# Output projection of the first block: seven block products in the place of eight, with sums of operands

## The chip, the cores and the metric

The kernel runs on one NeuronCore of a Trainium2 chip. The metric is the device time of one execution in microseconds (us), median over runs. Engines are named as in the profile: PE is TensorE (matmuls), DVE VectorE, ACT ScalarE, POOL GpSimd, SP SyncE, which only issues transfers here.

## The reference

Two transformer-like blocks over 512 tokens of width 1024, in float32. What matters here is the end of the first block: the mixed output `y` of its two attention branches is projected by `w_out` (1024 x 1024) and added to the residual `x`, and a normalised copy of the sum feeds a perceptron of hidden width 4096.

```python
y = gates[..., :D_MODEL] * y_a + gates[..., D_MODEL:] * y_b
x = x + y.astype(x.dtype) @ w_out[l]
h2 = rms_norm(x, norm_mlp_g[l])
x = x + jnp.square(jax.nn.relu(h2 @ w_up[l])) @ w_down[l]
```

## The kernel before

Each float32 operand of a matmul is split into a rounded part and its remainder (`hi` by a cast on ACT, `lo` by a subtraction on DVE), and a product is the sum of three matmuls: hi by hi, hi by lo, lo by hi. So a 128-row step of a 128 x 512 output block is three matmuls of 512 columns.

The heads of the second attention branch (`stick(h)`, h = 0 to 7) come one after the other; their work on DVE, ACT and PE is interleaved with matmuls of projections. When a head is done its row block of `y` is split into `T` (tiles `hh`, `hl`). The last head's split is the last thing that the output projection needs: in the trace it is the row L259 at 482.16.

The output projection is `wo(0)` and `wo(1)`: two halves of 512 columns, each over four token blocks (`tb`) of 128 rows and eight steps of 128 along the inner dimension. A half loads four weight tiles `wr` of 512 KB (`load_w`, L133), splits them (L137, L138), and for each token block runs 24 matmuls (L149 to L151) into one of two PSUM banks `mm`. `evac` loads the residual `x` of the token block (L1133) into a tile `qd` of the perceptron's space and adds the product (L1134). After the second half, `do(tb)` of `prep` normalises the finished token block: two squares with a running sum on ACT (L279), two small operations on POOL (L293, L115), two scalings on DVE (L283), then eight transposes of 128 x 128 on PE and their split (L258, L259) into `TM`, which `up(0)` reads. `up(0)` is run in two halves of 256 tokens.

The perceptron's pools (`st`, `b2`) are opened when those of the attention are closed; a tile in them takes space that attention tiles held, and its first write waits for their last readers. The tiles `wx` of this pool hold the first sums of weights of `down2`, which already runs as seven block products: `seven` computes a 2 x 2 block matrix product with seven block products, where some weight operands are sums of blocks. Such a sum is made by transfers: SP loads one block into a tile (`piece`, L181), and POOL issues a transfer that adds the next block to it (`plus`, L185).

A scheduler puts the instructions of each engine into one order ahead of time; an engine works its list strictly in that order. POOL's list holds both the adding transfers and the small operations of `do`.

Of the kernel before, what the change touches and what calls it, by code (L numbers as in the profile page):

```python
# [8 lines left out]
F32 = mybir.dt.float32  # L9
F32R = mybir.dt.float32r  # L10
# [3 lines left out]
ALU = mybir.AluOpType  # L14
# [3 lines left out]
P = 128  # L18
S = 512
D = 1024  # L20
NT = S // P
# [38 lines left out]
class Kern:  # L60
# [132 lines left out]
            nc.vector.tensor_tensor(lo, raw, hi.bitcast(F32), ALU.subtract)  # L193
        return [(hi[:, k, :], lo[:, k, :]) for k in range(2)]

    def seven(self, blk, aop, acc, wx):

        nc = self.nc
        X = []

        def w_of(name):
            out = []
            for q in range(2):
                if name == "X":
                    t = self.piece(blk(0, 0, q), wx())
                    self.plus(t, blk(0, 1, q))
                    X.append(t)
                elif name == "Y":
                    t = X[q]
                    self.plus(t, blk(1, 1, q))  # L210
                elif name == "Z":
                    t = X[q]
                    self.plus(t, blk(1, 0, q))
                elif name == "V":
                    t = self.piece(blk(0, 1, q))
                    self.plus(t, blk(1, 1, q))
                else:
                    t = self.piece(blk(int(name[0]), int(name[1]), q))
                out += self.split_w(t)
            return out  # L220

        def prod(ps, a, w, t, first):
            c = slice(t * P, (t + 1) * P)
            for k in range(4):
                (ah, al), (wh, wl) = (a[0][:, k, c], a[1][:, k, c]), w[k]
                kw = dict(stop=True, skip_group_check=True)
                nc.tensor.matmul(ps, ah, wh, start=(first and k == 0), **kw)  # L227
                nc.tensor.matmul(ps, ah, wl, start=False, **kw)  # L228
                nc.tensor.matmul(ps, al, wh, start=False, **kw)  # L229

        c = [None, None]
        x = [None, None]
        plan = [("X", "5", x, True, (1, 1, ALU.add)), ("11", "3", x, False, (0, 1, ALU.add)),
                ("00", "1", c, True, (0, 0, ALU.add)), ("Y", "6", c, False, (0, 1, ALU.subtract)),
                ("10", "2", x, True, (0, 0, ALU.add)), ("V", "7", c, False, (1, 1, ALU.subtract)),
                ("Z", "4", c, False, (1, 0, ALU.add))]
        for wn, an, bank, first, (i, j, op) in plan:
            w = w_of(wn)
            a = aop(an)
            for t in range(2):  # L240
                if first:
                    bank[t] = self.pmm() if bank is x else self.psum("xa")
                prod(bank[t], a, w, t, first)
                with self.tc.high_priority(EVP):
                    acc(i, t, j, bank[t], op)


    def new_T(self):
# [480 lines left out]
def block1(K, xd, prm, win, wout, wup, wdown, bif, gmix, gmlp, out, gnext):  # L729
# [383 lines left out]
    with ExitStack() as ctx:  # L1113
# [9 lines left out]

        def xt(tb, c):
            return x1[tb // 2][:, tb % 2 * 2 + c, :]
        TM = [[K.quad(F32R) for _ in range(2)] for _ in range(2)]
        do = K.prep(gmlp, wk2, wk2, TM)

        def wo(c):
            def evac(tb, ps):  # L1130
                w = slice(c * S, (c + 1) * S)
                t = xt(tb, c)
                nc.sync.dma_start(out=t, in_=xd[tb * P:(tb + 1) * P, w])  # L1133
                nc.vector.tensor_tensor(t, ps, t, ALU.add)  # L1134
                if c == 1:
                    do(tb, [xt(tb, 0), xt(tb, 1)])
            K.gemm_b(wout[:, c * S:(c + 1) * S], evac, x=K.pairs(T))
        wo(0)
        wo(1)
        K.hT = K.pairs(TM)  # L1140
        hid = {}

# [122 lines left out]
```

## Time and profile before

| | us |
|---|---|
| median of 3 runs (lowest, highest) | 1822.29 (1821.57, 1823.52) |
| the profiled execution's own time | 1821.35 |
| its span, first to last instruction | 1819.6 |
| PE busy in the span | 1781.9 (98%) |
| DVE busy | 1081.0 (59%) |
| ACT busy | 856.0 (47%) |
| POOL busy | 168.7 (9%) |

The profiled execution stands 0.94 us under the median of the runs. "Busy" counts a matmul from start to its modelled end, and matmuls overlap, so a busy PE is read by the distance of the starts of its rows.

### The profile page before, as it was taken

How to read it: one execution, taken by the hardware profiler on the slowest of the kernel's cores; microseconds unless marked ns; L12 is line 12 of the kernel's file. 1: busy time of each engine (PE TensorE's matmuls, PEld its weight loads, DVE VectorE, ACT ScalarE, POOL GpSimd, SP SyncE). 2: the span in 40 equal slices, each digit the busy share in tenths (PEclk: the TensorE clock that was granted, in tenths of full speed). 3: DMA queues.
4: the chain of work that ended last, by engine and by line, in shares of the span. 5: the costliest groups of instructions: out<-in, count | busy, mean ns of one | idle time of the engine just before them, and what ended most of it. 6: DMA issues, size and time to landing. Idle time of an engine off the chain costs nothing.

```text
span 1819.6 us, 29429 instructions
## 1 busy us (share of the span) xinstructions
PE 1781.9 (98%) x11600; PEld 1460.7 (80%) x11600; DVE 1081.0 (59%) x2186; ACT 856.0 (47%) x1701; POOL 168.7 (9%) x223
## 2 busy tenths in 40 slices
PE   7999999999899999999999999999999999999998
PEld 5777788787698888878888888878878888888886
DVE  5375445546555756588475676766364748577744
ACT  4556634343333433355344444766344335376641
POOL 1001111020000101012000001100120000111002
PEclk9999999999999999999999999999999999999999
DMA  7342332221533938378323223232342321332222
GB/s 217 72 105 77 92 93 65 75 93 46 162 117 93 232 106 217 93 185 250 108 82 94 81 85 121 93 116 81 106 147 88 121 76 60 122 128 76 82 70 93
DMA packets 114322, 201.05 MB, mean 110 GB/s; under 512 B 9600, under 2 KB 20224, under 8 KB 114184
## 3 DMA queue, kind: packets, MB, share of 16 engines
q1 hardware_dynamic: 105480, 182.40, 32.0%
q0 software_dynamic: 8704, 16.78, 5.2%
q8 instruction: 91, 1.49, 0.3%
q14 instruction: 47, 0.39, 0.1%
HBM read 184.45 MB, written 14.70 MB: 109 GB/s over the span
## 4 chain that ended last, share of the span: by engine, by line
PE 92%; DMA 3%; ACT 2%; DVE 2%; issue 0%; SPq 0%; POOL 0%; DVEq 0%; POOLq 0%; ACTq 0%
PE mm L151 23%; PE mm L150 23%; PE mm L149 23%; PE xc L638 2%; PE xa L602 2%; PE xa L228 1%; PE xa L227 1%; PE xa L229 1%; PE mm L227 1%; PE mm L228 1%; PE mm L229 1%; PE xc L1066 1%; PE xa L1048 1%; PE xb L624 1%; PE xc L498 1%; PE xa L443 1%
## 5 line engine op out<-in xcount | busy, mean ns | idle before, releaser
L149 PE MATMUL mm<-wh,hh 128*128 128x512 f32 (+1 forms) x896 | 349.6, 391 | 10.0 <-DVE qd L1134 4.8
L138 DVE TENSOR_TENSOR wl<-wr,wh 128x1024 fp32r<-128x1024 f32 (+1 forms) x240 | 288.6, 1211 | 114.8 <-PE mm L150 70.7
L150 PE MATMUL mm<-wl,hh 128*128 128x512 f32 (+1 forms) x896 | 349.4, 390 | 1.2 <-DVE wl L138 1.2
L151 PE MATMUL mm<-wh,hl 128*128 128x512 f32 (+1 forms) x896 | 348.6, 393 | 0.0
L137 ACT CAST wh<-wr 128x1024 fp32r<-128x1024 f32 (+1 forms) x240 | 246.7, 1037 | 120.6 <-PE mm L151 56.4
L149 PE MATMUL mm<-hh,wh 128*128 128x512 f32 x640 | 253.6, 396 | 1.4 <-ACT pg L803 1.4
L151 PE MATMUL mm<-hh,wl 128*128 128x512 f32 x640 | 252.3, 394 | 1.5 <-DVE wl L138 1.4
L150 PE MATMUL mm<-hl,wh 128*128 128x512 f32 x640 | 252.3, 394 | 0.0
L149 PEld LDWEIGHTS mm<-wh,hh 128*128 128x128 f32 x896 | 170.1, 190 | 44.5 <-DVE qd L1134 5.2
L150 PEld LDWEIGHTS mm<-wl,hh 128*128 128x128 f32 x896 | 170.1, 190 | 34.8 <-DVE wl L138 2.5
L151 PEld LDWEIGHTS mm<-wh,hl 128*128 128x128 f32 x896 | 168.8, 190 | 31.9 <-DVE hl L259 0.7
L151 PEld LDWEIGHTS mm<-hh,wl 128*128 128x128 f32 x640 | 120.2, 188 | 28.1 <-DVE wl L138 2.7
L149 PEld LDWEIGHTS mm<-hh,wh 128*128 128x128 f32 x640 | 120.2, 188 | 27.5 <-ACT pg L803 2.7
L150 PEld LDWEIGHTS mm<-hl,wh 128*128 128x128 f32 x640 | 120.4, 188 | 24.6
L115 POOL TENSOR_TENSOR sm<-sm,nhalf 128x4 f32<-128x4 f32 (+1 forms) x64 | 59.0, 922 | 506.6 <-DVE sm L507 329.9
L149 PE MATMUL mm<-qd,wh 128*128 128x512 f32 (+1 forms) x288 | 105.5, 366 | 0.0
L150 PE MATMUL mm<-qd,wh 128*128 128x512 f32 (+1 forms) x288 | 105.4, 366 | 0.0
L151 PE MATMUL mm<-qd,wl 128*128 128x512 f32 (+1 forms) x288 | 105.2, 365 | 0.0
L610 ACT ACTIVATE pg<-pg,sm 128x256 f32<-128x256 f32 (+1 forms) x128 | 60.9, 478 | 11.0 <-DVE sm L608 10.5
L1148 DVE TENSOR_TENSOR hr<-hr 128x512 f32<-128x512 f32 (+1 forms) x36 | 22.7, 631 | 69.4 <-ACT hr L1147 68.8
L149 PEld LDWEIGHTS mm<-qd,wh 128*128 128x128 f32 x288 | 54.3, 189 | 8.8
L151 PEld LDWEIGHTS mm<-qd,wl 128*128 128x128 f32 x288 | 54.3, 189 | 8.7
(310 smaller groups left out, 2983.5 us busy)
## 6 DMA issues: line engine op xcount, KB each, us to landing
wr<-in_w_in_dram SPq DMA_DIRECT2D x160, 512.0 KB, 5.0
wr<-in_w_out_dram SPq DMA_DIRECT2D x40, 512.0 KB, 3.5
wr<-in_w_up_dram SPq DMA_DIRECT2D x32, 512.0 KB, 5.2
wr<-in_w_down_dram SPq DMA_DIRECT2D x32, 512.0 KB, 5.9
wx<-in_w_down_dram POOLq DMA_DIRECT2D x24, 512.0 KB, 9.1
wx<-in_w_down_dram SPq DMA_DIRECT2D x8, 512.0 KB, 3.6
wr<-in_w_down_dram POOLq DMA_DIRECT2D x8, 512.0 KB, 8.0
zh<-pg SPq DMA_DIRECT2D x16, 256.0 KB, 2.1
```

The lines of the kernel that those rows point to most:

```text
L115: self.nc.gpsimd.tensor_tensor(y, ms, e, ALU.pow)
L137: nc.scalar.copy(hi, raw)
L138: nc.vector.tensor_tensor(lo, raw, hi.bitcast(F32), ALU.subtract)
L149: nc.tensor.matmul(ps, sh, mh, start=(k == 0), stop=False)
L150: nc.tensor.matmul(ps, sh, ml, start=False, stop=False)
L151: nc.tensor.matmul(ps, sl, mh, start=False, stop=(k == n - 1))
L227: nc.tensor.matmul(ps, ah, wh, start=(first and k == 0), **kw)
L228: nc.tensor.matmul(ps, ah, wl, start=False, **kw)
L229: nc.tensor.matmul(ps, al, wh, start=False, **kw)
L602: nc.tensor.matmul(psc[:, i, 2 * P - wi:], qT[p][e][:, t1 - P:t1], kT[kv][j][:, t1 - wi:t1], start=(j == 0), stop=(j == 1))
L610: nc.scalar.activation(prw, prw, AF.Exp, bias=pn[:, n:n + 1], scale=-1.0, accum_out=den[:, n:n + 1])
L638: nc.tensor.matmul(o, va[0][:, k, vv], pTs[e][k // 2][:, k % 2, w], start=(k == n), stop=(k < n or n == 0))
```

## The change

The output projection is computed by `seven` on 2 x 2 blocks: two halves of the tokens by two halves of the inner dimension, against two halves of the inner dimension by two halves of the columns. The new function `sides` makes the operands: products "1", "2" and "4" take halves of `T` as they are; for "5", "3", "6" and "7" it adds `hi` and `lo` back together for the four quarters (four operations of 128 x 1024 on DVE), forms four sums or differences of them (four more) and splits each (a cast on ACT and a subtraction on DVE of 128 x 1024) into tiles `sd` in the space that the perceptron's `hr` tiles take later. The residual is loaded into `x1` first, and each product is added to it or subtracted from it (`acc_o`). With `late=True` the order of the products is "1", "2", "5", "3", "6", "7", "4"; their weight operands are blocks 00, 10, the sum X (00 + 01), block 11, the sum Y (X + 11), the sum V (01 + 11) and the sum Z (Y + 10).

```diff
-    def seven(self, blk, aop, acc, wx):
+    def seven(self, blk, aop, acc, wx, late=False):
@@
+        if late:
+            plan = [plan[i] for i in (2, 4, 0, 1, 3, 5, 6)]
@@
+    def sides(self, T, pool, tmp):
+        nc = self.nc
+        def part(i, t):
+            return [a[i][:, :, 256 * t:256 * t + 256] for a in T]
+        ops = {"1": part(0, 0), "2": part(1, 0), "4": part(1, 1)}
+        raw = [q[:, :, 256 * e:256 * e + 256] for q in tmp for e in range(2)]
+        def whole(o, p):
+            nc.vector.tensor_tensor(o, p[0].bitcast(F32), p[1].bitcast(F32), ALU.add)
+        def keep(name, src):
+            o = pool()
+            self.split(o[:, 0], o[:, 1], src)
+            ops[name] = (o[:, 0], o[:, 1])
+        a11, a12, a21, a22 = raw
+        whole(a21, part(0, 1))
+        whole(a22, part(1, 1))
+        nc.vector.tensor_tensor(a22, a21, a22, ALU.subtract)
+        keep("5", a22)
+        whole(a11, part(0, 0))
+        whole(a12, part(1, 0))
+        nc.vector.tensor_tensor(a22, a22, a11, ALU.subtract)
+        nc.vector.tensor_tensor(a12, a22, a12, ALU.add)
+        keep("3", a12)
+        keep("6", a22)
+        nc.vector.tensor_tensor(a21, a11, a21, ALU.subtract)
+        keep("7", a21)
+        return ops
@@
+        for tb in range(NT):
+            for c in range(2):
+                nc.sync.dma_start(out=xt(tb, c), in_=xd[tb * P:(tb + 1) * P, c * S:(c + 1) * S])
+        sd = lambda: st.tile([P, 2, 4, 256], F32R, name=K.nm("sd"), tag="hr", bufs=4)
+        ops = K.sides(T, sd, [K.quad(), K.quad()])
         TM = [[K.quad(F32R) for _ in range(2)] for _ in range(2)]
         do = K.prep(gmlp, wk2, wk2, TM)
-        def wo(c):
-            def evac(tb, ps):
-                w = slice(c * S, (c + 1) * S)
-                t = xt(tb, c)
-                nc.sync.dma_start(out=t, in_=xd[tb * P:(tb + 1) * P, w])
-                nc.vector.tensor_tensor(t, ps, t, ALU.add)
-                if c == 1:
-                    do(tb, [xt(tb, 0), xt(tb, 1)])
-            K.gemm_b(wout[:, c * S:(c + 1) * S], evac, x=K.pairs(T))
-        wo(0)
-        wo(1)
+        due = {(tb, j): (2, 1)[tb // 2] if j == 0 else 2 for tb in range(NT) for j in range(2)}
+        def acc_o(i, t, j, ps, op):
+            tb = 2 * i + t
+            x = xt(tb, j)
+            nc.vector.tensor_tensor(x, x, ps, op)
+            due[tb, j] -= 1
+            if due[tb, j] == 0 and due[tb, 1 - j] == 0:
+                do(tb, [xt(tb, 0), xt(tb, 1)])
+        def blk_o(k, j, q):
+            r0 = k * S + q * 2 * P
+            return wout[r0:r0 + 2 * P, j * S:(j + 1) * S]
+        K.seven(blk_o, ops.get, acc_o, wx, True)
```

POOL's list behind the last small fill of the last head (`pg_3766`). Before: three adding transfers, all for `down2`, then the small operations of `do` for token blocks 0 and 1 (`sm_4029` and `sm_4031`, `sm_4082` and `sm_4084`).

```order
L1053 MEMSET pg_3766 128x1
L185 DMA wx_4715<-in_w_down_dram 128x2x512
L185 DMA wx_4722<-in_w_down_dram 128x2x512
L185 DMA wx_5282<-in_w_down_dram 128x2x512
L293 TENSOR_SCALAR sm_4029<-sm_4025,sm_4026 128x1
L115 TENSOR_TENSOR sm_4031<-sm_4029,nhalf 128x1
L293 TENSOR_SCALAR sm_4082<-sm_4078,sm_4079 128x1
```

POOL's list at the same place with the change. `wx_3950` and `wx_3957` hold the two halves of X, then of Y, then of Z; `wr_4125` is the second half of V; `sm_4059`, `sm_4061` and `sm_4098` belong to `do` of token blocks 0 and 1.

```order
L1088 MEMSET pg_3766 128x1
L185 DMA wr_4125<-in_w_out_dram 128x2x512
L185 DMA wx_3950<-in_w_out_dram 128x2x512
L185 DMA wx_3957<-in_w_out_dram 128x2x512
L185 DMA wx_4753<-in_w_down_dram 128x2x512
L185 DMA wx_3950<-in_w_out_dram 128x2x512
L185 DMA wx_3957<-in_w_out_dram 128x2x512
L185 DMA wx_3950<-in_w_out_dram 128x2x512
L185 DMA wx_3957<-in_w_out_dram 128x2x512
L185 DMA wx_4760<-in_w_down_dram 128x2x512
L328 TENSOR_SCALAR sm_4059<-sm_4055,sm_4056 128x1
L185 DMA wx_5320<-in_w_down_dram 128x2x512
L115 TENSOR_TENSOR sm_4061<-sm_4059,nhalf 128x1
```

The first two transfers into `wx` now make X where they made a sum for `down2`; one transfer of `down2` (`wx_4753`) stands between X and Y, and two (`wx_4760`, `wx_5320`, in the tiles that Z leaves) stand ahead of the small operations of token blocks 0 and 1.

DVE's list with the change, from the split of the last head (`hl_3804` from `pg_1314`) to the first remainder of X (`wl_3954`). `qd_3840` and `qd_3841` hold the sums of operands, `qd_3830` the residual of token blocks 0 and 1; `xa_3882`, `xa_3896` are the two banks of product "1", `mm_3922` and `mm_3936` those of product "2"; `sd_3845` is operand "5". Before, the first of these rows was followed by the additions L1134.

```order
L294 TENSOR_TENSOR hl_3804<-pg_1314,hh_3802 128x512
L260 TENSOR_TENSOR qd_3841<-hh_3801,hl_3803 128x4x256
L260 TENSOR_TENSOR qd_3841<-hh_3802,hl_3804 128x4x256
L260 TENSOR_TENSOR qd_3840<-hh_3801,hl_3803 128x4x256
L260 TENSOR_TENSOR qd_3840<-hh_3802,hl_3804 128x4x256
L1173 TENSOR_TENSOR qd_3830<-qd_3830,xa_3882 128x512
L270 TENSOR_TENSOR qd_3841<-qd_3841 128x4x256
L1173 TENSOR_TENSOR qd_3830<-qd_3830,xa_3896 128x512
L1173 TENSOR_TENSOR qd_3830<-qd_3830,mm_3922 128x512
L278 TENSOR_TENSOR qd_3841<-qd_3840,qd_3841 128x4x256
L1173 TENSOR_TENSOR qd_3830<-qd_3830,mm_3936 128x512
L294 TENSOR_TENSOR sd_3845<-qd_3841,sd_3845 128x1024
```

All eight sums and the splits of the operands stand behind the last head's split.

DVE's list with the change, later: `wl_4129` is the remainder of V's second half, `wl_4160` and `wl_4165` those of Z; the additions that empty the banks follow.

```order
L193 TENSOR_TENSOR wl_4129<-wr_4125,wh_4128 128x1024
L193 TENSOR_TENSOR wl_4160<-wx_3950,wh_4159 128x1024
L193 TENSOR_TENSOR wl_4165<-wx_3957,wh_4164 128x1024
L1173 TENSOR_TENSOR qd_3830<-qd_3830,mm_3978 128x512
L1173 TENSOR_TENSOR qd_3830<-qd_3830,xa_3882 128x512
L138 TENSOR_TENSOR wl_4250<-wr_4247,wh_4249 128x1024
L1173 TENSOR_TENSOR qd_3830<-qd_3830,xa_3896 128x512
```

The second remainder of Z stands ahead of the addition that empties bank `xa_3882` of Y, the bank that V's first matmul writes next.

PE's list with the change, at the end of X (`wh_3960`, `sd_3845`): two matmuls of Y (`wh_4031`, into `xa_3882` and `xa_3896`) stand ahead of the product "3" of block 11 (`wh_3994`).

```order
L228 MATMUL mm_3978<-wl_3961,sd_3845 128x512
L229 MATMUL mm_3978<-wh_3960,sd_3845 128x512
L227 MATMUL xa_3882<-wh_4031,sd_3855 128x512
L227 MATMUL xa_3896<-wh_4031,sd_3855 128x512
L227 MATMUL mm_3964<-wh_3994,sd_3852 128x512
L228 MATMUL mm_3964<-wl_3995,sd_3852 128x512
```

The matmuls of block 11 come behind the first two of Y.

## Rows read from the trace of the kernel before

**Rows 1.** The page: span, busy time by engine, and the shares of the chain that ended last.
```profile
span 1819.6 us, 29429 instructions
PE 1781.9 (98%) x11600; PEld 1460.7 (80%) x11600; DVE 1081.0 (59%) x2186; ACT 856.0 (47%) x1701; POOL 168.7 (9%) x223
...
PE 92%; DMA 3%; ACT 2%; DVE 2%; issue 0%; SPq 0%; POOL 0%; DVEq 0%; POOLq 0%; ACTq 0%
```

**Rows 2.** PE in order of time, from the last head's last matmuls to the start of `up(0)`. Columns: start, us; duration, us; engine, line, operation, output and inputs, shape, count; in brackets the idle time before and what ended it.
```profile
478.96 1.06 PE L1066 MATMUL xc<-pg,pg 128*128 128x256 f32 x4
482.18 0.50 PE L149 MATMUL mm<-wh,hh 128*128 128x512 f32 x1 [2.16 <-ACT hh L258]
...
483.21 0.63 PE L151 MATMUL mm<-wh,hl 128*128 128x512 f32 x2
488.59 0.80 PE L149 MATMUL mm<-wh,hh 128*128 128x512 f32 x1 [4.75 <-DVE qd L1134]
...
490.04 0.63 PE L149 MATMUL mm<-wh,hh 128*128 128x512 f32 x1
490.47 0.63 PE L150 MATMUL mm<-wl,hh 128*128 128x512 f32 x1
...
494.57 0.39 PE L151 MATMUL mm<-wh,hl 128*128 128x512 f32 x1
494.80 0.40 PE L149 MATMUL mm<-wh,hh 128*128 128x512 f32 x1
...
525.61 0.39 PE L151 MATMUL mm<-wh,hl 128*128 128x512 f32 x1
...
526.19 0.36 PE L149 MATMUL mm<-qd,wh 128*128 128x256 f32 x1
```

**Rows 3.** Two stretches, busy time of each engine (and instructions), then the granted clock of PE, the share of the 16 DMA engines and GB/s.
```profile
489.00:494.30 5.30, 5.30 (x13) 4.05 (x13) 0.19 (x1) 0.29 (x2) 0.00 (x0) 0.50 1.09 255
494.30:526.20 31.90, 31.90 (x153) 26.58 (x151) 16.81 (x21) 13.33 (x24) 4.48 (x7) 1.00 0.46 132
```

**Rows 4.** DVE in order of time (columns as in rows 2): the split of the last head, the first additions and a weight split.
```profile
482.16 0.69 DVE L259 TENSOR_TENSOR hl<-pg,hh 128x512 fp32r<-128x512 f32 x1 [0.68 <-ACT hh L258]
487.85 1.34 DVE L1134 TENSOR_TENSOR qd<-mm,qd 128x512 f32<-128x512 f32 x2 [4.99 <-DMA qd<-in_x_dram]
...
498.18 1.23 DVE L138 TENSOR_TENSOR wl<-wr,wh 128x1024 fp32r<-128x1024 f32 x1 [0.44 <-PE mm L150]
```

**Rows 5.** Transfers issued by SP in order of time (columns as in rows 2).
```profile
469.16 0.93 SPq L266 DMA_DIRECT2D wk<-in_norm_mlp_g_dram  x2
480.05 1.83 SPq L181 DMA_DIRECT2D wx<-in_w_down_dram  x2
481.93 5.48 SPq L1133 DMA_DIRECT2D qd<-in_x_dram  x8
487.77 0.38 SPq L181 DMA_DIRECT2D wx<-in_w_down_dram  x1
```

**Rows 6.** Adding transfers issued by POOL in order of time (columns as in rows 2).
```profile
484.27 1.39 POOL L185 DMA_DIRECT2D wx<-in_w_down_dram  x1 [24.78 <-PE mm L151]
487.62 1.21 POOL L185 DMA_DIRECT2D wx<-in_w_down_dram  x1 [1.96 <-DMA wx<-in_w_down_dram]
499.42 1.20 POOL L185 DMA_DIRECT2D wx<-in_w_down_dram  x1 [10.59 <-DMA wx<-in_w_down_dram]
```

**Rows 7.** The view of transfers, asked for a window around each issue of rows 6, in the same order. Last column: us from issue to landing.
```profile
wx<-in_w_down_dram POOLq DMA_DIRECT2D x1, 512.0 KB, 9.6
...
wx<-in_w_down_dram POOLq DMA_DIRECT2D x1, 512.0 KB, 10.2
...
wx<-in_w_down_dram POOLq DMA_DIRECT2D x1, 512.0 KB, 7.7
```

**Rows 8.** The same view for adding transfers of the first `down2`: two that were issued singly (at 574.28 and 592.13), then four that were issued in a row (from 600.62 to 604.48).
```profile
wx<-in_w_down_dram POOLq DMA_DIRECT2D x1, 512.0 KB, 6.0
...
wx<-in_w_down_dram POOLq DMA_DIRECT2D x1, 512.0 KB, 7.6
...
wr<-in_w_down_dram POOLq DMA_DIRECT2D x1, 512.0 KB, 8.0
...
wr<-in_w_down_dram POOLq DMA_DIRECT2D x1, 512.0 KB, 8.7
...
wx<-in_w_down_dram POOLq DMA_DIRECT2D x1, 512.0 KB, 10.9
...
wx<-in_w_down_dram POOLq DMA_DIRECT2D x1, 512.0 KB, 13.7
```

**Rows 9.** The same view for a plain load of 512 KB by SP, issued at 522.12.
```profile
wr<-in_w_up_dram SPq DMA_DIRECT2D x1, 512.0 KB, 3.6
```

**Rows 10.** ACT, then POOL, then DVE in order of time: a cast of a weight tile, a square of a token block's half, the two small operations of `do`, and its two scalings.
```profile
498.41 1.05 ACT L137 CAST wh<-wr 128x1024 fp32r<-128x1024 f32 x1 [9.11 <-PE mm L151]
508.65 0.63 ACT L279 ACTIVATE wk<-qd 128x512 f32<-128x512 f32 x1 [5.11 <-DVE qd L1134]
...
509.48 0.29 POOL L293 TENSOR_SCALAR sm<-sm,sm 128x1 f32<-128x1 f32 x1 [8.86 <-ACT wk L279]
509.86 0.57 POOL L115 TENSOR_TENSOR sm<-sm,nhalf 128x1 f32<-128x1 f32 x1
...
510.47 1.41 DVE L283 SCALAR_TENSOR_TENSOR wk<-qd,sm,wk 128x512 f32<-128x512 f32 x2 [1.85 <-POOL sm L115]
```

## The prediction

> **What bounds the kernel now.** I read the page first: PE is busy for 98% of the span and holds 92% of the chain that ended last [rows 1], so time is lost or gained where PE's list moves. Then PE's own rows around the output projection [rows 2]. PE runs out of work when the last head ends: it stands for 2.16 us until that head is split, runs six matmuls to 483.84 (483.21 + 0.63), and stands for 4.75 us more, put down to the first addition on DVE. That addition waited for the residual, whose loads SP issued from 481.93, behind two loads of 512 KB at 480.05 [rows 4, 5]. From 488.59 matmuls start every 0.43 us, from 494.3 every 0.23 us [rows 2]; the granted clock was 0.50, which is 1.2 GHz, up to 494.3 and 1.00, 2.4 GHz, behind it [rows 3]. So the 13 slow matmuls of rows 3 cost 13 x 0.20 = 2.6 us. From 488.59 to the first matmul of `up(0)` at 526.19 PE never waits again. This stretch is what the change replaces, and both kernels have run 48 of their matmuls when it begins.
>
> **What it removes.** Eight block products of 24 matmuls become seven: 192 become 168, and 24 x 0.227 us (the distance of starts in rows 2) = **5.4 us** go. That is the whole gain in view; the eight transposes of each token block, the split of `T` and the loads' bytes of `w_up` stay.
>
> **What it adds, in the order of PE's list.** Products "1" and "2" need `T` alone and fill the 48 matmuls that `wo(0)` filled; they end at 483.84 as before. Then PE needs X.
>
> *Operand "5"* comes from DVE. Behind the last split (482.16 + 0.69 = 482.85) stand four sums of 128 x 1024. No row shows that operation on such tiles; the nearest is a weight split, 1.22 us apart [rows 4]: 487.7. The addition behind them waits for the residual anyway (487.85), so the sums are hidden by that wait, and would cost 4.9 us without it. Then four additions of 0.67, two more sums and the operand's split: 487.85 + 2.7 + 3.6 = 494.1. The lower bound of a sum is the 0.69 of half as many elements, which would give about 491.5.
>
> *The weights X* come later. Its two loads stand where two of `down2` stood, and wait for the same last readers. So POOL issues the additions at 484.27 and 487.62 [rows 6], and they land 9.6 and 10.2 us later [rows 7]: 493.9 and 497.8. I add 1 us to each, because the two loads of the norm's gains, at 469 before [rows 5], now wait for space that the last head's transposes read, which end just ahead of its last matmuls at 478.96 [rows 2]; that puts half a megabyte just ahead of X (bounds 0 and 2). A cast of 1.05 [rows 10] gives 496.0 for X's first matmul against 488.59: **+7.4 us** (bounds +5.5, by operand "5" alone, and +10). The low clock there costs what it cost before. The remainder is ready at 497.2 and that of the second half at 501.1, behind two more sums: **+0.3**. X ends at 504.3.
>
> The Trainium skill ("DMA: Bandwidth & Descriptors", Anatomy of one DMA) prices a transfer issued by GpSimd at about 2.0 us plus its bytes over 436 GB/s, 3.2 us for 512 KB. Rows 7 and 8 show 6.0 to 13.7 us for these adding ones, and the measurement decides; by the page's price X would wait for operand "5" alone.
>
> *Y* is X plus a block, added in place, so its transfer is issued only after X is split, and in POOL's list behind the one of `down2` that now stands between: that one waits for its own load and was issued at 499.42 [rows 6]; with the 1 us, 500.4. Y's two follow at 1.2 us each: 501.6 and 502.8. In a row of such transfers the second landed after 8.7 us, the third after 10.9 [rows 8]: 510.3 and 513.7. Before PE may do the 24 matmuls of block 11, which need no sum by transfer, its list has two matmuls of Y, so it cannot fill the gap. With the cast, PE goes on at 511.35: **+7.0 us** (bounds 3.3, landing after 6.0, and 12, after 13.7).
>
> A pause of this length has a price of its own: the pauses of 2.16 and 4.75 us, with six matmuls between, were followed by a clock of 0.50 for 5.7 us. I take the same 13 matmuls at 0.20 us: **+2.6** (bounds 0 and 2.6). Y and block 11, 48 matmuls, end at 511.35 + 10.9 + 2.6 = 524.9.
>
> *V* has long been added, but its first matmul writes a bank that DVE must empty first, and DVE's list has Z's second remainder ahead of that addition. Z's second transfer is issued when Y's second half is split (513.7 + 1.05 + 1.2 = 516.0); singly issued ones landed after 6.0 and 7.6 us [rows 8]; with 7.6, 523.6, and with cast, split and two additions 527.2: **+2.4** (bounds 0.7 and 5.6).
>
> *Token blocks 0 and 1* must be normalised between the halves of Z. Their small operations on POOL stand behind two additions for `down2`, whose loads can start only when Z's two halves are split (522.5 and 525.9) and take 3.6 us or a little more [rows 9]: the second is issued at about 529.9, the power follows at 531.1 + 0.57, the scalings of two blocks, two weight splits and one addition bring DVE to 537.6 (durations of rows 4 and 10). PE is there at 527.2 + 8.1 + 0.7 = 536.1: **+1.5** (bounds 0 and 3). The same work was hidden by 24 matmuls per token block before.
>
> *Behind Z* six groups of transposes are left for `up(0)` where three were, which moves PE work but adds none. The last block's chain (addition 0.69, squares 1.3, small operations 0.9, scalings 1.4, and weight splits of 1.2 ahead of some of these in DVE's list) takes about 7 us; PE has 26 matmuls of half width and five groups of transposes, about 5: **+2.0** (bounds 0 and 4). It replaces a chain that had no wait in rows 2.
>
> Hidden at no cost: six more additions to the residual, six more weight tiles and four operand splits on DVE and ACT (59% and 47% busy [rows 1]); their cover is the same stretch, and where it is gone they are counted above. Behind `up(0)` the lists are the same, and its later sums are landed long before use.
>
> **Sum.** -5.4 + 7.4 + 0.3 + 7.0 + 2.6 + 2.4 + 1.5 + 2.0 = +17.8 us on the profiled execution's 1821.35, so 1839.2. The median of the runs stands 0.94 above that execution: **1840**. Lower bounds together give +4, upper ones +32.
>
> **Rivals.** *Only the first wait counts.* Y's first transfer lands after 6 to 7 us, the pause is short and the clock holds: -5.4 + 7.4 + 0.3 + 3.3 + 0.7 + 1 = +7, 1829. For it: singly issued transfers do land so fast. Against it: three are issued in a row here, and every row of rows 8 that followed another took longer.
>
> *The transfers are in time*, and this ends on the other side, not slower. If X lands within about 8 us of its issue and each later sum before PE asks, only operand "5" is waited for: -5.4 + 5.5 = 0, 1822. It decides at a landing of X's first half by 492 and of Y's by 503. For it: PE's list is made so that this would fit. Against it: 493.9 and 497.8 were measured for the same transfers at the same place, and Y cannot be issued before 501. A gain beyond 0.2% (3.6 us) would need cheaper sums on DVE too.
>
> The Trainium skill's price of 3.2 us (same section) would put this rival first. No row here shows an adding transfer that fast.
>
> *The queue builds up.* Transfers of Y and Z land as the last of the row of four did (13.7): Y +12, V +5.6, Z +3: about +28, 1850. For it: SP issues four loads of `w_up` in the same stretch. Against it: Z's are issued apart.
>
> **How the numbers follow.** The forecast (1832 to 1848) has 0.62, the short wait 0.18, the transfers in time 0.07, the long queue 0.13. From 1829 to 1849 holds the forecast, about two thirds of the short wait and a third of the long queue, some 0.8. A change of 0.2%, 3.6 us, is about what a measurement of this kernel can tell from none. Slower by more than that: 0.91; within it 0.06; faster 0.03, all from the case where transfers are in time.
>
> **What the profile will show.** Right: an idle time of PE of about 12 us ahead of X, one of 5 to 9 us ahead of Y's first matmul (put down to the cast on ACT) with a granted clock of 0.50 behind it, 1 to 5 us ahead of V and again within Z, and `up(0)` starting near 540 in place of 526. Wrong: Y's matmuls following X without a pause; or POOL's additions landing within 5 us; or PE's idle time before X ended by DVE's operand "5" and not by X's cast.

## The result, and the profile after

The changed kernel takes **1841.53 us** (median of 4 runs, 1840.87 to 1843.47) where the kernel before took 1822.01 beside it: a ratio of 1.0107, 95% interval 1.009 to 1.0125. It is 19.5 us slower; 1840 was forecast. Its profiled execution took 1841.06, 19.7 more than that of before.

The page of the changed kernel, to be read against [rows 1]:

```profile
span 1839.3 us, 29453 instructions
PE 1781.6 (97%) x11576; PEld 1459.9 (79%) x11576; DVE 1105.5 (60%) x2210; ACT 866.2 (47%) x1711; POOL 178.7 (10%) x231
...
PE 88%; DMA 4%; ACT 3%; DVE 2%; issue 1%; POOL 1%; SPq 0%; DVEq 0%; POOLq 0%; ACTq 0%
```

PE has as much busy time as before, although 24 matmuls are gone (11600 - 11576), and its share of the chain fell from 92% to 88%: the time is in waits. PE in order of time, against [rows 2]:

```profile
482.62 0.50 PE L227 MATMUL mm<-wh,hh 128*128 128x512 f32 x1 [2.16 <-ACT hh L293]
497.48 1.22 PE L227 MATMUL mm<-wh,sd 128*128 128x512 f32 x2 [13.19 <-ACT wh L192]
...
505.11 0.39 PE L229 MATMUL mm<-wh,sd 128*128 128x512 f32 x1
511.67 1.22 PE L227 MATMUL xa<-wh,sd 128*128 128x512 f32 x2 [6.17 <-ACT wh L192]
...
515.63 0.39 PE L228 MATMUL mm<-wl,sd 128*128 128x512 f32 x1
...
529.17 0.72 PE L227 MATMUL xa<-wh,sd 128*128 128x512 f32 x1 [4.54 <-DVE qd L1173]
...
532.66 0.39 PE L229 MATMUL xa<-wh,sd 128*128 128x512 f32 x1
...
542.91 0.40 PE L149 MATMUL mm<-qd,wh 128*128 128x256 f32 x2
...
547.57 0.66 PE L321 MATMUL xa<-ident,wk 128*128 128x128 f32 x4 [0.31 <-DVE qd L294]
...
550.32 0.66 PE L321 MATMUL xa<-ident,wk 128*128 128x128 f32 x4 [0.61 <-DVE qd L294]
```

The matmuls that follow the last head's split start at 482.62 (482.18 before, a shift of 0.44 that is there from 160 us on). Then PE stands 13.19 us for X's cast, 6.17 for Y's, 4.54 for the bank that DVE must empty ahead of V, and has short waits among the transposes in `up(0)`, which starts at 542.91 in place of 526.19. The stretches behind these pauses, against [rows 3] (granted clock third from the end):

```profile
497.40:501.40 4.00, 3.88 (x8) 2.65 (x9) 3.59 (x3) 1.64 (x5) 0.92 (x2) 0.50 0.30 71
502.60:505.40 2.80, 2.80 (x13) 2.07 (x11) 2.80 (x4) 2.80 (x4) 1.50 (x2) 1.00 1.02 170
511.60:514.80 3.20, 3.13 (x7) 2.48 (x8) 1.82 (x2) 0.16 (x2) 1.22 (x1) 0.50 0.87 236
529.10:532.10 3.00, 2.93 (x7) 2.38 (x8) 1.65 (x2) 2.01 (x6) 1.11 (x3) 0.52 0.88 203
```

Each pause is followed by a spell at about 0.50, 1.2 GHz, before the clock is 1.00, 2.4 GHz, again. POOL's adding transfers in order of time, against [rows 6], and where they landed (X, X, Y, Y, and Z's second; last column: us from issue to landing), against [rows 7]:

```profile
486.26 1.20 POOL L185 DMA_DIRECT2D wx<-in_w_out_dram  x1 [19.56 <-DMA wx<-in_w_out_dram]
488.48 1.19 POOL L185 DMA_DIRECT2D wx<-in_w_out_dram  x1 [1.02 <-DMA wx<-in_w_out_dram]
...
501.21 3.00 POOL L185 DMA_DIRECT2D wx<-in_w_out_dram  x2
...
517.32 1.21 POOL L185 DMA_DIRECT2D wx<-in_w_out_dram  x1 [2.86 <-DVE wl L193]
```

```profile
wx<-in_w_out_dram POOLq DMA_DIRECT2D x1, 512.0 KB, 10.1
...
wx<-in_w_out_dram POOLq DMA_DIRECT2D x1, 512.0 KB, 11.9
...
wx<-in_w_out_dram POOLq DMA_DIRECT2D x1, 512.0 KB, 9.3
...
wx<-in_w_out_dram POOLq DMA_DIRECT2D x1, 512.0 KB, 11.6
...
wx<-in_w_out_dram POOLq DMA_DIRECT2D x1, 512.0 KB, 8.1
```

So X landed at 496.36 and 500.39, Y at 510.55 and 514.57, Z's second half at 525.44. Y's two are the row with x2, the second issued at 503.02. DVE: the remainder of operand "5", then Z's second remainder and the addition that empties V's bank:

```profile
493.30 1.22 DVE L294 TENSOR_TENSOR sd<-qd,sd 128x1024 fp32r<-128x1024 f32 x1
...
526.60 1.23 DVE L193 TENSOR_TENSOR wl<-wx,wh 128x1024 fp32r<-128x1024 f32 x1 [4.50 <-ACT wh L192]
...
528.34 0.68 DVE L1173 TENSOR_TENSOR qd<-qd,xa 128x512 f32<-128x512 f32 x1
```

**A measure of the stretch.** The program's time moves by several us from one execution to the next (the kernel before took 1819.20 to 1828.02 us beside e1, e1b, e2 and e5), so the experiments are read from two rows that all traces share: the first matmul behind the last head's split, and the first cast in the first `down2` that follows 4.3 us of idle time on ACT. This is the latter in the kernel before, and then in the changed one:

```profile
600.12 1.06 ACT L192 CAST wh<-wx 128x1024 fp32r<-128x1024 f32 x1 [4.31 <-PE xa L229]
```

```profile
620.13 1.06 ACT L192 CAST wh<-wx 128x1024 fp32r<-128x1024 f32 x1 [4.30 <-PE xa L229]
```

Before, the two lie 600.12 - 482.18 = 117.94 apart, after 620.13 - 482.62 = 137.51: the stretch costs **19.6 us**, the whole loss. The same for the experiments, in us (the last column is the median's ratio to the kernel before, with its interval):

| kernel | first matmul behind the split | X's first matmul, behind that | cast in `down2` | stretch against before | ratio |
|---|---|---|---|---|---|
| before | 482.18 | 6.41 | 600.12 | 0 | 1 |
| changed | 482.62 | 14.86 | 620.13 | +19.6 | 1.0107 (1.009 to 1.0125) |
| e1, no sums of weights | 482.52 | 14.32 | 609.51 | +9.1 | 1.0048 (1.003 to 1.0065) |
| e1b, only X and V summed | 484.16 | 13.77 | 614.91 | +12.8 | 1.0055 (1.0038 to 1.0073) |
| e2, no sums of operands | 484.09 | 13.58 | 618.61 | +16.6 | 1.0088 (1.0069 to 1.0107) |
| e10, neither | 483.48 | 6.65 | 600.24 | -1.2 | 1.0002 (0.9993 to 1.0011) |
| e11, no residual loads | 482.64 | 11.56 | 612.94 | +12.4 | 1.0066 (1.0052 to 1.0079) |
| e16, Z without its sum | 482.76 | 13.94 | 622.15 | +21.5 | 1.0111 (1.0094 to 1.0128) |
| e17, Y without its sum | 482.67 | 14.24 | 610.35 | +9.7 | 1.0072 (1.0057 to 1.0087) |
| e5, sums made near 20 to 100 us | 497.24 | 10.07 | 617.21 | +2.0 | 1.0075 (1.0056 to 1.0093) |
| e5b, sums made between projections | 483.51 | 10.08 | 603.16 | +1.7 | 1.0018 (1.0008 to 1.0028) |

### The profile page after: what moved, and what is told of

The parts are those of the page before. It is cut to its first block, busy times and chain, and to the rows that moved or that the text cites. A ratio compares the mean times of both kernels' runs of the same rounds, so it can differ in the third digit from the quotient of the medians.

```text
span 1839.3 us, 29453 instructions
## 1 busy us (share of the span) xinstructions
PE 1781.6 (97%) x11576; PEld 1459.9 (79%) x11576; DVE 1105.5 (60%) x2210; ACT 866.2 (47%) x1711; POOL 178.7 (10%) x231
## 4 chain that ended last, share of the span: by engine, by line
PE 88%; DMA 4%; ACT 3%; DVE 2%; issue 1%; POOL 1%; SPq 0%; DVEq 0%; POOLq 0%; ACTq 0%
PE mm L150 21%; PE mm L151 21%; PE mm L149 21%; PE xa L227 2%; PE xc L673 2%; PE xa L228 2%; PE xa L229 2%; PE xa L637 2%; DMA wx<-in_w_out_dram 1%; PE mm L227 1%; PE mm L229 1%; PE mm L228 1%; PE xc L1101 1%; PE xa L1083 1%; PE xb L659 1%
## 5 line engine op out<-in xcount | busy, mean ns | idle before, releaser
L138 DVE TENSOR_TENSOR wl<-wr,wh 128x1024 fp32r<-128x1024 f32 (+1 forms) x232 | 278.9, 1212 | 114.9 <-PE mm L150 68.7
L149 PE MATMUL mm<-wh,hh 128*128 128x512 f32 (+1 forms) x832 | 323.1, 389 | 3.5 <-ACT hh L712 1.3
L150 PE MATMUL mm<-wl,hh 128*128 128x512 f32 (+1 forms) x832 | 323.7, 389 | 0.8 <-DVE wl L138 0.8
L151 PE MATMUL mm<-wh,hl 128*128 128x512 f32 (+1 forms) x832 | 322.5, 391 | 0.0
L137 ACT CAST wh<-wr 128x1024 fp32r<-128x1024 f32 (+1 forms) x232 | 238.4, 1037 | 114.0 <-PE mm L151 46.3
L149 PEld LDWEIGHTS mm<-wh,hh 128*128 128x128 f32 x832 | 157.4, 189 | 34.4 <-ACT wh L137 2.1
L150 PEld LDWEIGHTS mm<-wl,hh 128*128 128x128 f32 x832 | 157.2, 189 | 31.5 <-DVE wl L138 2.1
L151 PEld LDWEIGHTS mm<-wh,hl 128*128 128x128 f32 x832 | 156.1, 189 | 28.9 <-DVE hl L294 0.5
L149 PEld LDWEIGHTS mm<-qd,wh 128*128 128x128 f32 x288 | 54.2, 189 | 9.0 <-ACT qd L293 0.2
L150 PEld LDWEIGHTS mm<-qd,wh 128*128 128x128 f32 x288 | 54.3, 189 | 8.7
```

Source lines behind the costliest of these rows:

```text
L137: nc.scalar.copy(hi, raw)
L149: nc.tensor.matmul(ps, sh, mh, start=(k == 0), stop=False)
L150: nc.tensor.matmul(ps, sh, ml, start=False, stop=False)
L151: nc.tensor.matmul(ps, sl, mh, start=False, stop=(k == n - 1))
```

## Experiments

### Which sums hold PE: e1, e1b, e2, e10

The theory of the prediction: PE waits for the adding transfers. The rival: it waits for the sums of operands on DVE.

e1 (X, Y, V and Z are their first block):

```diff
+        plus = (lambda t, s: None) if late else self.plus
...
-                    self.plus(t, blk(0, 1, q))
+                    plus(t, blk(0, 1, q))
...
```

> The changed kernel (1841.5 us) without the adding transfers of the output projection: X, Y, V and Z are only their first block, so the sums of weights are left out; loads, splits, matmuls, operand sums and PE's order stay. Theory (PE waits for the adding transfers): X then waits for operand "5" alone, which was ready at 494.5, against 497.5 (-2.9); the wait ahead of Y (-6.2), the wait ahead of V (-4.5) and the two spells of half clock behind them (-1.5, -1.7) go: 1841.5 - 16.8 = 1824.7, between 1821 and 1829. Rival (the operand sums on DVE, or PE's new order, hold PE): no more than the 2.9 us go, 1838 to 1842, and the waits ahead of Y and V stay.

Measured: 1832.73, between the theory's range and the rival's. The waits ahead of Y and V are gone (short ones are left between the two halves of V and of Z), but that ahead of X is not. PE of e1, and DVE of e1 ahead of X:

```profile
496.84 0.76 PE L228 MATMUL mm<-wh,sd 128*128 128x512 f32 x1 [12.64 <-DVE qd L1174]
...
522.44 0.50 PE L228 MATMUL xa<-wh,sd 128*128 128x512 f32 x1 [1.54 <-DVE qd L1174]
...
529.59 0.50 PE L228 MATMUL xa<-wh,hh 128*128 128x512 f32 x1 [0.97 <-DVE qd L1174]
```

```profile
489.14 0.69 DVE L1174 TENSOR_TENSOR qd<-qd,xa 128x512 f32<-128x512 f32 x1 [0.27 <-DMA qd<-in_x_dram]
...
494.88 1.22 DVE L193 TENSOR_TENSOR wl<-wx,wh 128x1024 fp32r<-128x1024 f32 x1
496.02 0.68 DVE L1174 TENSOR_TENSOR qd<-qd,mm 128x512 f32<-128x512 f32 x1
```

The wait of 12.64 us is now put down to DVE: with the weights there early, their remainders (L193) stand in DVE's list ahead of the additions that empty the banks of product "2", where X wants to write. DVE works without a pause from 489.14 to 496.02. Of the 16.8 us expected, the stretch gave 10.5. The expectation took the order of the lists as given, but with the transfers gone the scheduler also moved rows of PE, ACT and DVE (so too in e1b, e10, e11 and e17; e2 keeps PE's order but for one matmul, e16 that of PE and DVE). So a single run shows what this kernel does without these transfers, not the price of the transfers alone.

e1b keeps the adding transfers of X and V:

```diff
+        plus = self.plus
+        skip = (lambda t, s: None) if late else self.plus
...
-                    self.plus(t, blk(1, 1, q))
+                    skip(t, blk(1, 1, q))
...
```

> The changed kernel with X and V summed by adding transfers, but Y and Z taken as X (the sums Y and Z are left out). Theory (each wait is that of its own transfer): the 13.2 us ahead of X stay, the waits ahead of Y and V and the half clock behind them go: 1841.5 - 6.2 - 1.5 - 4.5 - 1.7 = 1827.6, between 1825 and 1831. Rival (a wait that goes is taken by the next thing that is late, as operands "3" and "6" on DVE): at least half of the 13.9 us stays, 1834 or more.

Measured: 1834.34, the rival's side: 6.8 us of the stretch came back, not 13.9. In place of the waits ahead of Y and V PE now has four of 0.7 to 1.7 us for operands and additions, two of them with a spell of half clock behind (1.7 and 1.6 us).

e2 takes the operands from the halves of `T`:

```diff
+        ops.update({"5": part(1, 1), "3": part(0, 1), "6": part(0, 1), "7": part(1, 0)})
+        return ops
         a11, a12, a21, a22 = raw
```

> The changed kernel with operands "5", "3", "6" and "7" taken from the halves of T as they are: the eight sums and four splits of operands on ACT and DVE are left out, the adding transfers of the weights stay. Theory (PE waits for the adding transfers): X starts at about 497 as before, Y and V wait as they did: 1839 to 1842. Rival (the operand chain behind the last head holds PE): X starts near 490 and the total falls by 5 us or more, to 1836 or less.

Measured: 1840.02, as the theory has it. PE of e2:

```profile
497.67 1.22 PE L227 MATMUL mm<-wh,hh 128*128 128x512 f32 x2 [11.92 <-ACT wh L192]
...
514.36 0.73 PE L227 MATMUL xa<-wh,hh 128*128 128x512 f32 x2 [2.50 <-ACT wh L192]
...
527.81 0.77 PE L227 MATMUL xa<-wh,hh 128*128 128x512 f32 x1 [7.71 <-DVE qd L1175]
```

X is still waited for, by its cast: it starts 13.58 us behind the split (14.86 in the changed kernel), so the transfers alone suffice to hold PE. What Y gained in this run (2.50), V's wait (7.71) took back. So each chain alone keeps X late, and e10, which is e1 and e2 together, asks whether there is a third.

> The changed kernel without either kind of sum: weights X, Y, V, Z are only their first block, and operands "5", "3", "6", "7" are halves of T (both kinds of sums are left out). Theory (ahead of X two things are late at the same time, the adding transfers and DVE's list, and each alone hides behind the other): X starts at 490.5 to 493, behind the residual at 488.6 and the additions that empty its banks, against 497.5; with the waits ahead of Y and V and the half clock behind them gone this is 1841.5 - 6 - 6.2 - 4.5 - 3.2 = 1821.6, and up to 4 us more for short waits on DVE: 10 to 20 us below the changed kernel. Rival (a third thing, the residual's loads or the banks, holds X near 496 anyway): as without the sums of weights alone, 1831 or more.

Measured: 1823.2, no different from the kernel before. PE of e10:

```profile
490.13 0.77 PE L228 MATMUL mm<-wh,hh 128*128 128x512 f32 x1 [4.50 <-DVE qd L1176]
...
513.02 0.50 PE L228 MATMUL xa<-wh,hh 128*128 128x512 f32 x1 [1.03 <-DVE qd L1176]
```

X starts 6.65 us behind the split, as in the kernel before (6.41), held by the residual and the first additions. There is no third chain ahead of X, and without the two kinds of sums the loss is gone. Without any sum the stretch gains 1.2 us: of the 5.4 us of 24 matmuls the rest goes to two waits of 1.1 us for DVE, 1.0 of transposes in `up(0)`, and to gaps that no row names.

### Why an adding transfer takes 10 us: e11

```diff
-        for tb in range(NT):
-            for c in range(2):
-                nc.sync.dma_start(out=xt(tb, c), in_=xd[tb * P:(tb + 1) * P, c * S:(c + 1) * S])
...
+            if (tb, j) in seen:
+                nc.vector.tensor_tensor(x, x, ps, op)
+            else:
+                nc.vector.tensor_copy(x, ps)
+                seen.add((tb, j))
```

> The changed kernel without the eight loads of the residual (256 KB each) that SP issues behind X's two loads: the first addition to each tile becomes a copy, so the residual is left out; all else stays. Theory A (an adding transfer takes 10 us at this place because it shares the DMA engines with these loads): X's two additions land 6 to 8 us behind their issue in place of 10.1 and 11.9, X starts 2 to 3.5 us earlier, then by operand "5" at about 494, and Y, issued behind X's split, goes forward with it: 1836 to 1840. Theory B (an adding transfer has this length of its own, when two are issued within 3 us): the landings stay at 9.5 to 12 us and the time at 1840 to 1843.

Measured: 1835.61, just below theory A's range. X's two transfers in e11 (issued at 485.44 and 488.23), then PE, then ACT:

```profile
wx<-in_w_out_dram POOLq DMA_DIRECT2D x1, 512.0 KB, 7.6
...
wx<-in_w_out_dram POOLq DMA_DIRECT2D x1, 512.0 KB, 7.7
```

```profile
494.20 1.22 PE L227 MATMUL mm<-wh,sd 128*128 128x512 f32 x2 [9.55 <-ACT wh L192]
...
509.19 0.80 PE L227 MATMUL mm<-wh,sd 128*128 128x512 f32 x1 [7.54 <-ACT sd L293]
```

```profile
506.20 1.04 ACT L192 CAST wh<-wx 128x1024 fp32r<-128x1024 f32 x1 [3.55 <-DMA wx<-in_w_out_dram]
...
508.09 2.94 ACT L293 CAST sd<-qd 128x1024 fp32r<-128x1024 f32 x3
```

Theory A: 7.6 and 7.7 us, where X's landings took 9.2 to 12.7 in the changed kernel, e1b, e2, e16 and e17, which have these loads; so some 2 us or more of each landing were the loads of the residual beside it, and X starts at 494.20, 3.3 us earlier. Y, issued from 495.70, is no longer named by a wait of PE. In its place stands 7.54 us for operand "3", a cast on ACT whose source DVE had done at 501.66. But ACT's list, which the scheduler moved, has the casts of both halves of Y ahead of it, and the second waited 3.55 us for its transfer: Y's transfer holds PE still, through ACT's list.

### The bank ahead of V: e16, e17

e16 leaves out Z's adding transfers; DVE and PE keep the order of the changed kernel row by row.

```diff
-                    self.plus(t, blk(1, 0, q))
+                    late or self.plus(t, blk(1, 0, q))
```

> The changed kernel without Z's two adding transfers (Z is taken as Y, so this sum is left out); the lists of DVE and PE stay in the order of the changed kernel. Theory (V waits for a bank that DVE empties only behind Z's second remainder, which waits for Z's transfer): the 4.54 us ahead of V and the half clock behind it (1.7) go, the waits ahead of X (13.2) and Y (6.2) stay: 1841.5 - 4.5 - 1.7 = 1835.3, between 1834 and 1837. Rival (DVE reaches the bank late for its own work, the transfer is not what counts): at least 3 us of the wait stay, 1838 or more.

Measured: 1845.19 (the kernel before took 1824.38 beside it), a time on the rival's side; the stretch is 1.9 us dearer than the changed kernel's. PE and DVE of e16 behind Y:

```profile
527.29 0.47 PE L227 MATMUL xa<-wh,sd 128*128 128x512 f32 x1 [0.18 <-DVE qd L1173]
...
537.23 0.66 PE L321 MATMUL xb<-ident,wk 128*128 128x128 f32 x4 [1.08 <-DVE wk L318]
539.62 0.80 PE L227 MATMUL xa<-wh,hh 128*128 128x512 f32 x1 [1.74 <-DVE qd L1173]
```

```profile
533.96 1.42 DVE L318 SCALAR_TENSOR_TENSOR wk<-qd,sm,wk 128x512 f32<-128x512 f32 x2 [2.97 <-POOL sm L115]
```

The theory's mechanism is right nevertheless: V waits 0.18 us in place of 4.54. What was wrong is that time would be saved by it. PE then stands 1.08 and 1.74 us between the halves of Z, with a spell at 0.50 behind (12 matmuls, 2.4 us), for token blocks 0 and 1, whose scaling on DVE waited 2.97 us for POOL's small operations, behind two additions for `down2` that were issued at 530.40 and 532.06. From Y's first matmul to the cast in `down2` it is 622.15 - 513.88 = 108.27 us here and 620.13 - 511.67 = 108.46 in the changed kernel: the wait moved and nothing was gained. The 1.9 us more lie ahead of Y, whose unchanged transfers landed after 11.0 and 13.0 us in this run (9.3 and 11.6 above). So much does a landing vary.

e17 leaves out Y's instead, by the same edit at `blk(1, 1, q)`; here the scheduler also moved rows of PE, ACT and DVE.

> The changed kernel without Y's two adding transfers (Y is taken as X, so this sum is left out), with Z's kept. Theory (Y's transfers also put Z's back, as Z is added into the same tiles): the waits ahead of Y and of V both go, Z's transfers being issued some 12 us earlier; what is left is X's wait and the short waits for operands on ACT and DVE that stood there in the run without Y and Z (1834.3): 1833 to 1836. Rival (V's wait is Z's transfer's own affair): only 6.2 - 1.3 + 1.5 us go and the wait ahead of V stays at 3 us or more, 1835.1 plus 0 to 2, with V's wait to be seen in the trace.

Measured: 1837.5 (1824.38 before, beside it), 1.5 us above the theory's range and 0.4 above the rival's; the stretch is 9.8 us cheaper, and the rest of the program dearer by some 3. In this trace PE waits 0.71 us ahead of Y and not ahead of V (0.78 between V's halves, 1.74 between Z's), so the theory's mechanism holds: Z's transfers, issued at 505.56 and 506.69 in place of 513.24 and 517.32, are in time when Y's don't stand ahead. e1b, with Z's transfers gone too, is 3.1 us dearer than e17: about what the half clock behind its short waits costs (3.3 us), where the granted clock stayed 1.00 in e17. So a difference of 3 us between two such runs tells nothing of one transfer.

### Looking for a version that beats both: e5, e5b, e9b, e12, e13

e5 makes the four sums early in DRAM and loads them plainly:

```diff
+        for name, first, more in (("X", b(0, 0), b(0, 1)), ("V", b(0, 1), b(1, 1)),
+                                  ("Y", "X", b(1, 1)), ("Z", "Y", b(1, 0))):
+            d = K.dp.tile([S, S], F32, name=f"ws{name}")
+            nc.sync.dma_start(out=d, in_=sums[first] if isinstance(first, str) else first)
+            nc.gpsimd.dma_start(out=d, in_=more, accum_op=ALU.add)
...
+                if sums and name in sums:
+                    t = self.piece(sums[name][q * 2 * P:(q + 1) * 2 * P, :])
```

> The changed kernel with the four sums of weights X, V, Y, Z made early, near 350 us, in DRAM: SP copies a block there, POOL adds the next to it, and the output projection loads each sum plainly by SP into weight tiles; nothing is left out. Theory: as without the adding transfers, X waits for operand "5" (ready at 494.5), the waits ahead of Y and V and the half clock behind them go: 1841.5 - 16.8 = 1824.7, between 1821 and 1829; the early transfers cost nothing, since nothing waits for them there. Rival (the place, not the kind of transfer, is what is late, as there are six weight tiles of 512 KB only): PE stands ahead of Y and V for their plain loads, 1833 or more.

Measured: 1837.67, not in the theory's range. The stretch is what was hoped, +2.0, but the early transfers, issued from 23 to 85 us and not near 350, were not free. PE's waits from 60 to 200 us in e5:

```profile
PE mm L151 <- DVE wl L138: 14.4, 1, 14.4
```

They fell together with loads of weights near 80 us, and one remainder came 14.4 us late. e5b therefore gates the copies by tiles of a later stage:

```diff
...
+            nc.sync.dma_start(out=d[:P, :4], in_=gate_by[:, :4])
+            nc.sync.dma_start(out=d, in_=first)
...
```

> The changed kernel with the four sums of weights made in DRAM as before, but between the projections of the second branch (each copy waits for a tile of that stage) and from the four blocks directly, so that they do not fall together with the loads near 80 to 140 us, where PE stood 14.4 us in the run before this one. Theory: the stretch of the output projection stays as in that run, where up(0) started 0.9 us ahead of the kernel before once the 15.15 us of delay that were there at 464 us are taken off: 1821, between 1818 and 1826, 15 to 22 us below the changed kernel. Rival (the sums cost their time wherever they stand, as they take 4 copies and 5 additions of 1 MB): 1830 or more.

Measured: 1826.49, half a us above the theory's range: 15 us below the changed kernel but 0.18% above the one before. The stretch is +1.7. X's first matmul in e5b waits for DVE alone:

```profile
493.59 0.77 PE L229 MATMUL mm<-wh,sd 128*128 128x512 f32 x1 [8.32 <-DVE qd L1184]
```

e9b puts product "4" third, with two banks of its own:

```diff
-            plan = [plan[i] for i in (2, 4, 0, 1, 3, 5, 6)]
+            plan = [plan[i] for i in (2, 4, 6, 0, 1, 3, 5)]
+            plan[2] = ("Z", "4", [None, None], True, (1, 0, ALU.add))
...
```

> As the kernel with sums made between the projections, and product "4" (weights Z), which needs T alone, is moved from the last to the third place, into two banks of its own; its sum goes to the residual by itself, and so two more additions are needed for token blocks 2 and 3. Nothing is left out. Theory: 24 matmuls fill the time in which PE stands ahead of X for DVE (8.4 us in the first run with early sums): 24 x 0.227 = 5.4 us less than without, 1816, between 1811 and 1820, so below the kernel before. Rival (the two more additions on DVE and two more banks put X's start back by as much, or the transposes of the last head wait for the banks): no gain over the kernel with sums made late, 1820 or more.

Measured: 1831.11, worse; its cast in `down2` comes 6.4 us later than before's, e5b's 3.0. PE of e9b:

```profile
501.07 0.77 PE L229 MATMUL mm<-wh,sd 128*128 128x512 f32 x1 [11.88 <-DVE qd L1187]
```

Nine matmuls of "4" stand ahead of the last head's last two, which start at 482.75; the residual's loads follow 3 us later than in e5b, the additions behind them too, and X waits 11.88 us.

e12 and e13 (with "4" early) put operand "5" first on DVE, two sums on POOL, and "5" into banks of its own:

```diff
...
-                    bank[t] = self.pmm() if bank is x else self.psum("xa")
+                    bank[t] = self.psum("xa") if bank is c else self.psum("xb") if late and bank is x else self.pmm()
...
+            whole(a11, part(0, 0), nc.gpsimd)
...
```

> The kernel with sums of weights made between the projections (1826.5 us), and three edits to DVE's part: the first operand's sums stand ahead of the others, two of the four sums of hi and lo go to POOL (128 x 1024 there is shown by no run so far), and product "5" gets two banks of its own, so that X need not wait until DVE has emptied those of product "2". Nothing is left out. Theory (ahead of X only DVE's list is left): behind the last head's split, near 484.1, come a weight remainder, two sums and one difference, 1.15 each, and ACT's cast, 1.05: X starts at 489.8 to 491.5 in place of 493.6, so 1822 to 1825. Rival (sums on POOL are slow, or slow DVE down while they run, or the additions that wait for the residual still stand ahead): X at 493 or later, 1826 or more.

> The same, and product "4" in the third place as in the run in which that was tried, now in banks that no transpose of the last head uses. Nothing is left out. Theory: X starts no later than without, and 24 matmuls, 5.4 us, no longer stand behind it; two more additions of 0.6 on DVE in the tail: 4 us under the other kernel of this call, 1818 to 1821, below the kernel before. Rival (as in the first run of this product order, matmuls of "4" stand ahead of the last head's own in PE's list and put its end and the residual's loads back): no gain over the other kernel of this call.

Measured: 1827.64 and 1829.97, the rivals' side both times; X starts at 494.9 and 499.6. Behind the split it is 10.07 us in e12, as in e5b (10.08). POOL, then DVE of e12, and the same of e13:

```profile
485.57 2.36 POOL L264 TENSOR_TENSOR qd<-hh,hl 128x1024 f32<-128x1024 f32 x1 [12.97 <-DVE hl L299]
```

```profile
486.05 2.96 DVE L193 TENSOR_TENSOR wl<-wr,wh 128x1024 fp32r<-128x1024 f32 x1 [0.56 <-PE mm L230]
...
491.93 0.69 DVE L1187 TENSOR_TENSOR qd<-qd,xa 128x512 f32<-128x512 f32 x1 [0.65 <-DMA qd<-in_x_dram]
```

```profile
488.72 5.12 POOL L267 TENSOR_TENSOR qd<-hh,hl 128x1024 f32<-128x1024 f32 x2
```

```profile
489.80 5.13 DVE L193 TENSOR_TENSOR wl<-wr,wh 128x1024 fp32r<-128x1024 f32 x1 [1.16 <-ACT wh L192]
```

A remainder of 1.22 us took 2.96 and 5.13, and ended 1.1 us behind POOL's sums (485.57 + 2.36 and 488.72 + 5.12): DVE stood while POOL ran, so what POOL took over was not saved. In e12 the first addition (491.93) waited 0.65 us more for the residual, so POOL's sums alone are not shown to be what holds X there. No version here beats the kernel before.

## Why the prediction was right, and where it was not

The forecast and its main mechanism held: PE's pauses ahead of X, Y and V are the ones that were named, each put down to the engine that was named. The wait that was named within Z did not come, and `up(0)` starts at 542.91, not near 540. Term by term, forecast and measured:

- **X later**: +7.4 and 497.48 - 488.59 - 0.44 = +8.45. The first transfer landed after 10.1 us as taken, but was issued 1.55 later than in [rows 6] (486.26 - 484.27 - 0.44), where 1 us was taken for the gains' loads. The 24 matmuls of X, 497.48 to 505.11, hold 23 x 0.227 = 5.2 and 2.4 us of half clock, as before: the +0.3 for the second half did not come.
- **Y**: +7.0 and 6.17. Issues at 501.21 and 503.02 (501.6 and 502.8 forecast), landings 9.3 and 11.6 (8.7 and 10.9).
- **Half clock**: +2.6, taken for one pause. The nine steps from 511.67 to 515.63 took 3.96 in place of 2.04, +1.9; and the eight behind V's pause, 529.17 to 532.66, 3.49 in place of 1.82, +1.7. The second spell was not in the sum.
- **V**: +2.4 and 4.54. Z's second transfer was issued at 517.32, not 516.0: Y's second half, whose remainder on DVE it waits for, landed at 514.57, not 513.7, and 0.4 us went between the engines. It landed after 8.1, not 7.6.
- **Token blocks 0 and 1**: +1.5 and 0. DVE's second pair of scalings ended at 538.26 (537.6 forecast), but PE came to the transposes at 539.02, not 536.1, since V's wait and the half clock behind it were longer than in the sum. The mechanism is real, as e16 showed; here V's wait ran over the same time, and of two such waits only the later counts.
- **Tail in `up(0)`**: +2.0; its waits are 0.31, 0.39 and 0.61, +1.3.

With the -5.4 and the 0.2 less of half clock at X, these are 18.5 of the 19.6; 1.1 us are in gaps that I have not assigned. That 1840 came so near is in part luck: V, the half clock and X cost 2.1, 1.0 and 0.8 us more than the sum has, token blocks, Y and the tail 1.5, 0.8 and 0.7 less.

One bound of the prediction is added up wrongly: Y's lower one, 3.3, leaves out the cast (501.6 + 6.0 + 1.05 - 504.3 is 4.35). With it the lower bounds together give +5, and the first rival about 1831.

What the runs showed wrong is in a rival, and in what was held to be hidden. *The transfers are in time* was priced at 0: X 5.5 us later for operand "5" alone, against the 5.4 us of a block product. In e5b, whose plain loads land before the last head ends, X starts only 3.7 us later, and yet the stretch costs 1.7: behind X's start PE waits for DVE for 0.45 us, 1.02 us and, among the transposes in `up(0)`, 1.2 us. The last two belong to what the sum has as token blocks and tail, and the rival left out; e10 has such waits without any sum (1.03, 1.12 and 1.0). In e1 the weights' remainders move ahead on DVE, X starts 7.9 us later than before (14.32 - 6.41), and the stretch costs 9.1. So the rival's price was 1.7 to 9.1. The shares of 59% and 47%, by which more work on DVE and ACT was held to be hidden, are averages of the whole span; ahead of X, DVE's list has no gap (e1).

The expectations of the experiments repeat this. The pauses ahead of Y and V were put down to transfers rightly, but a wait's length was taken for what its removal would return: of 13.9 us half came back in e1b, of 6.2 nothing in e16. The forecast did not need these figures, and so it held.

## What to carry to other kernels

A block product less is a gain of 24 matmuls, 5.4 us, at most (1.2 us of it were left in e10, without any sum), and it has to pay for the pauses that its sums put between engines: look for the point where all work that needs no sum has run out, and count everything that must be ready there. The releaser that the trace names is only the last of several; before moving it away, read the second one's time off its own rows, and test both together, as single removals gave 3.0 and 10.5 us here, and both 20.8. The releaser can also be a stand-in: in e11 PE waited for a cast that stood in ACT's list behind another one, which waited for a transfer. Where two waits run over the same time, only the later one counts.

## What was not expected of the hardware

- An adding transfer of 512 KB landed after 5.8 to 13.0 us at this place; with the eight loads of 256 KB away, X's took 7.6 and 7.7 in place of 10.1 and 11.9 (e11).
- The clock fell behind a pause of 4.54 us too, for eight matmuls, as behind 6.17 for nine; in e16 pauses of 1.08 and 1.74, with four transposes between, were followed by twelve matmuls at 0.43 us (granted clock 0.50). In e17 a pause of 1.74 us at the same place, with none of 1.08 ahead of the transposes, was followed by a clock of 1.00.
- DVE stood while POOL added two operands: 1.22 us became 2.96 and 5.13. The Trainium skill ("Trainium Architecture — The Big Picture", What this means for kernel authors) says that these two engines share a pair of ports under an exclusive lock; these rows agree with that.
